# Loads and differences of ya and yb spread over the second in-projection, score banks held through the gated projections, and two low parts made later

## The chip, the cores and the metric

One core of a Trainium2 chip runs the whole kernel as one program. The metric is the device time of an execution in microseconds. TensorE is PE, VectorE DVE, ScalarE ACT, GpSimd POOL and SyncE SP; SP issues nearly all DMAs.

## The reference

A hybrid decoder block over 2048 positions of width 1024, all in f32:

```python
ada = (silu(c) @ w_ada + b_ada); shift, scale, gate = split(ada, 3)
h = rms(x, g_pre) * (1 + scale) + shift
q, k, v, z_a, u_b, v_b, z_b, g_logits = split(h @ w_in, SPLIT_IDX)
y_a = sliding_window_attention_with_sinks(rope(q), rope(k), v, sinks) * silu(z_a)
y_b = chunked_spatial_gating(gelu(u_b), gelu(v_b), ln_v_g, ln_v_b, w_s, b_s) * silu(z_b)
gate_a, gate_b = split(sigmoid(g_logits), 2)
merged = gate_a * (y_a @ w_proj_a) + gate_b * (y_b @ w_proj_b)
x = x + gate * rms(merged @ w_out, g_post)
```

q has 8 heads of 64, k and v have 2; the window is 128; u_b, v_b and z_b are 512 wide, the gate logits 2048. The spatial gating multiplies chunks of 128 positions of the layer-normalised v_b with a causal 128 x 128 matrix.

## The kernel before

**Products.** Every large product is made in parts of f32r: each operand is split into a high part (a rounded copy, made on ACT) and a low part (operand minus high part, made on DVE), and a tile takes three matmuls per 128 of depth: high by high, high by low, low by high (`mm3`, its matmul at L168). Blocks of products use seven multiplications instead of eight, with sums and differences of the quarters of both operands. One such multiplication is a *slot*: 12 matmuls of 128 x 512 into one PSUM bank, or six and six into two. There are 382 slots. `step` (L229) runs one; `later(n, f)` hangs an operation on the slot n further on, ahead of its matmuls, or behind them with `post`. Hooks are thus an order written by hand: the instructions of every engine stand in the order in which the hooks ran, and each engine and queue works through its own in order.

**Stages.** The rows are handled in two halves, s = 0 and s = 1. Each half has an in-projection of 133 slots. Beside its matmuls run, on hooks, the evacuation of its blocks, the layer norm of v_b (`ln_step`, L847: one load of vb at L850, transposes on PE at L856 four slots later), the transposes of k and v (L924, evacuated by ACT at L928), the rotary tables (`load_rope`, L791: 16 loads of 64 KB at L798), the spatial gating (loads of vn at L971, matmul at L977), and eight attention blocks (loads of q and k at L1019 and L1022, scores at L1038 and L1039 into the bank pair s, values at L1088). Then come the projections of y_a and y_b with their gates: for the rows of s = 0 in *pairs* (`Pair`), Pair 0 and Pair 1 of seven slots each, Pairs 2 and 3 interleaved in 14, and then `run_all`'s loop over j of 32 slots for the rows of s = 1, whose operands `T[0]` to `T[3]` are plain parts of ya and yb (`yab`). The out projection ends the kernel with 56 slots. The slots of s = 1 are counted here from the start of its in-projection: Pair 0 is 133 to 139, Pair 1 140 to 146, Pairs 2 and 3 147 to 160, the loop 161 to 192.

**Moving tiles.** `T[p]` is the moving operand of multiplication p, four k parts with a high and a low half. `t_load(T, p, n, srcs)` (L373) issues four loads of 256 KB into tiles of tag x, makes the four high parts on ACT (L384) at slots n, and the four low parts on DVE (L388, by `sub`, L151) at slots n + 1. Four of the seven operands of the pairs are sums and differences of quarters of the s = 0 part of ya and yb: `y_step(i)` (L1212) loads four x tiles of 256 KB, subtracts on POOL (`psub`, L154) into tiles of tag S, and stores four results to pT in DRAM. `presum` does the like for weights (four loads, POOL sums, four stores to sS), `o_step` for the output weights (stores to oT). `gate_step` and `gate_end` make the gate row rg.

**Buffers.** Tag x has 10 buffers, S 4, raw (loaded weights) 8, W (split weights) 4, T 7, e 6, m 4, q 5. PSUM holds the banks X, Y, Z, W, a rotating pair b, and one tile s of two banks. Weights are loaded some eight slots ahead of their use and split three slots ahead (L216 on ACT, L151 on DVE).

**Gating.** After a product of the pairs the block's banks are combined by adds on DVE (L157) into tiles e, multiplied with the gate (`gated`, L1236) and merged.

Of the kernel before, what the change touches and what calls it, by code (L numbers as in the profile page):

```python
# [8 lines left out]
F32 = mybir.dt.float32  # L9
# [6 lines left out]
P = 128  # L16
# [12 lines left out]
NPAIR = 19  # L29
# [26 lines left out]
def hybrid_block(ctx: ExitStack, tc: tile.TileContext, xt, x, wada, wgate, wI, wP, wO,  # L56
# [14 lines left out]
    def nm(s):  # L71
        uid[0] += 1
        return f"{s}_{uid[0]}"
# [22 lines left out]
    def bank():  # L96
        return pb.tile([P, 512], F32, tag="b", name=nm("b"))
# [124 lines left out]
    def later(n, f, post=False):  # L222
        hooks.setdefault((slot[0] + n, post), []).append(f)
# [77 lines left out]
    def p_quads(n):  # L301

        return {f"A{f + 1}{k + 1}": wP[2 * n + f][:, :, 256 * k : 256 * (k + 1)].rearrange("a p c -> p a c")
                for f in range(2) for k in range(2)}
# [65 lines left out]
    def t_new():  # L370
        return T_new().rearrange("p (a b c) -> p a b c", a=2, b=4)

    def t_load(T, p, n, srcs):  # L373

        rs = []
        for src in srcs:
            rs.append(flat("x"))
            sp.dma_start(rs[-1], src)

        def high(k0):  # L380
            if k0 == 0:
                T[p] = t_new()
            for kt in (k0, k0 + 1):
                act.copy(T[p][:, 0, kt, :], rs[kt])  # L384

        def low(k0):
            for kt in (k0, k0 + 1):
                sub(T[p][:, 1, kt, :], rs[kt], T[p][:, 0, kt, :].bitcast(F32))  # L388
        for i in range(2):
            later(n, lambda i=i: high(2 * i), i == 1)  # L390
            later(n + 1, lambda i=i: low(2 * i), i == 1)


    class Block:
# [767 lines left out]
    def o_step(kt):  # L1162
        hs = []
        for k in (kt, kt + 4):
            for h in range(2):
                hs.append(flat("x"))
                sp.dma_start(hs[-1], wO[k][:, h * 512 : (h + 1) * 512])
        keep_T(oT, kt, hs, False, 3)
# [43 lines left out]
    def y_step(i):  # L1212
        hs = []
        for k in (i % 2, i % 2 + 2):
            for h in range(2):
                hs.append(flat("x"))
                sp.dma_start(hs[-1], (ya_s, yb_s)[i // 2][h][:, k, :])
        keep_T(pT, i, hs, False, 3)
# [24 lines left out]
    def run_all():  # L1243
        nonlocal T

        for s in range(NS):
            uz = [{} for _ in range(4)]
            kinds = [lambda: ev_vb(s, 0), lambda: ev_vb(s, 2), lambda: ev_kv(s), lambda: ev_q(s, 0), lambda: ev_g(s, 0),
                     lambda: ev_q(s, 2), lambda: ev_za(s, 0), lambda: ev_za(s, 2)]
            kinds += [lambda c=c: ev_uz(s, c, uz[c]) for c in range(4)]  # L1250
            kinds += [lambda j=j: ev_g(s, j) for j in range(1, 8)]

            if s == 0:
                later(19, setup_sgu)
                later(22, zero_heads)
            later((18, 12)[s], lambda s=s: load_rope(s))
            for i in range(8):
                later((22, 17)[s] + 3 * i, lambda i=i: ln_step(s, i))
            for c in range(4):
                later(52 + 7 * c, lambda c=c: uz_load(s, c, uz[c]))  # L1260
            for i in range(8):
                for off, post, f in att_block(s * 8 + i):
                    later(62 + 8 * i + off, f, post)
            if s == 0:
                for i in range(8):
                    later(30 + 5 * i, lambda i=i: h1_stats(i))
                later(71, h1_rstd)
                for kt in range(4):
                    later(76 + 10 * kt, lambda kt=kt: h1_step(kt))
                for i in range(NLAST):  # L1270
                    later(91 + 10 * i, lambda i=i: presum(NPAIR - NLAST + i, wI_quads(NPAIR - NLAST + i)))
            else:
                for i in range(4):
                    later(6 + 3 * i, lambda i=i: y_step(i))
                for i in range(2):
                    later((1, 82)[i], lambda i=i: presum(NPAIR + i, p_quads(2 + i)))
                for kk in range(KT):
                    later(30 + 7 * kk, lambda kk=kk: gate_step(kk))
                for h in range(2):
                    later(87 + 4 * h, lambda h=h: gate_end(h))  # L1280
                for kt in range(4):
                    later(90 + 7 * kt, lambda kt=kt: o_step(kt))

            n0 = 0
            if s == 0:
                n0 = NFIRST
                S = pS.tile([P, 2, 512], F32, tag="s", name=nm("s"))
                bks = [two_banks(BK["X"], BK["W"]), two_banks(BK["Y"], BK["Z"]), two_banks(S[:, 0, :], S[:, 1, :])]
                blks = [Block(bks[i], kinds[i](), "mme"[i]) for i in range(NFIRST)]
                def second_half():  # L1290
                    rstd(1, BK["Z"])
                    ada_row(1, range(2))
                    rstd_out(1, BK["W"])
                    sum_to(2 * NFIRST + 2)
                    want(NFIRST)
                    ada_row(1, range(2, 8))
                    for i in range(6):
                        t_part(1, i)
                        if i == 2:
                            low_now()  # L1300
                            ada_rows_out(1)
                        elif i == 4:
                            want(NFIRST + 1)

                def second_rows():
                    low_now()
                    ada_fin(1)
                    want(NFIRST + 3)
                    for i in range(2):
                        t_part(2, i)  # L1310
                    low_now()
                    
                def fetch_all():
                    cur["cap"] = 1 << 30
                later(2, second_half, True)
                later(3, fetch_all, True)
                later(3, second_rows, "mid")
                later(3, lambda: sp.dma_start(mcpt, mcp))
                later(3, lambda: sp.dma_start(snk8, sinks.broadcast_to([P, 8])))
                later(9, lambda: dve.tensor_scalar(out=snk8, in0=snk8, scalar1=1.0 / SM, scalar2=None, op0=ALU.mult))  # L1320
                for i in range(2, 6):
                    later(3 + (i > 2), lambda i=i: t_part(2, i), i != 3)
                for p in range(3, 7):
                    for i, (n, post) in enumerate(((-3, True), (-3, True), (-2, False), (-2, True), (-1, False), (-1, True))):
                        later(3 * p + n, lambda p=p, i=i: t_part(p, i), post)
                for p in range(7):
                    for i in range(NFIRST):
                        w = w_get()
                        step(lambda: blks[i].run(p, w, T))
            for n in range(n0, NPAIR - NLAST):  # L1330
                blk = Block(BK, kinds[n]())
                for p in range(7):
                    w = w_get()
                    step(lambda: blk.run(p, w, T))
            bks = [two_banks(BK["X"], BK["W"]), two_banks(BK["Y"], BK["Z"])]
            blks = [Block(bks[i], kinds[NPAIR - NLAST + i]()) for i in range(NLAST)]
            nT = [None] * 7
            for p in range(7):
                if s == 0:
                    t_load(nT, p, 2, hT[p])  # L1340
                else:
                    t_load(nT, p, 2, p_src(p))
                for i in range(NLAST):
                    w = w_get()
                    step(lambda: blks[i].run(p, w, T))
            T = nT

        def banks():
            S = pS.tile([P, 2, 512], F32, tag="s", name=nm("s"))
            return S[:, 0, :], S[:, 1, :], bank(), bank()  # L1350

        for n in range(2):
            c = banks()
            blk = Pair(n, (BK, {"X": c[0], "Y": c[1], "Z": c[2], "W": c[3]}))
            for p in range(7):
                w = w_get()
                step(lambda: blk.run(p, w, T))
        c = banks()
        blks = [Pair(2, (two_banks(BK["X"], BK["W"]), two_banks(BK["Y"], BK["Z"]))),
                Pair(3, (two_banks(c[0], c[1]), two_banks(c[2], c[3])))]  # L1360
        nT = [None] * 7
        for p in range(7):
            if p < 4:
                t_load(nT, p, 2, yab(1, p))
            if p == 6:
                g_load(1, 0)
            for i in range(2):
                w = w_get()
                step(lambda: blks[i].run(p, w, T))
# [171 lines left out]
```

## Time and profile before

| what | value |
|---|---|
| time, median of 3 runs | 1227.82 us (1227.78 to 1229.73) |
| profiled execution | 1228.62 us |
| its span | 1226.9 us, so 1.72 us lie around it |
| mean granted clock of TensorE | 0.991 |
| busy: PE, DVE, ACT, POOL | 1199.8, 863.2, 631.8, 348.0 us |
| moved by DMA | 311.47 MB, mean 254 GB/s |

Times are of one profiled execution. PE's sum of busy time includes matmuls at a lower clock, so a loss can show as idle time or as long matmuls; the clock in a stretch of time tells the second. A row of the timeline gives start, length, engine, line, operation and operands, the count of like instructions run together, and in brackets the idle time ahead with what ended it. SPq is SP's DMA queue. A row of a table by stretches gives for each engine the busy time and count, and then the granted clock, the DMA engines' mean share and GB/s.

### The profile page before, as it was taken

To read this page: it belongs to the slowest core of one execution; us is meant where nothing else is said; L and a number is where in the kernel's file an instruction comes from. 1 tells how busy PE (TensorE), PEld (TensorE's weight loads), DVE (VectorE), ACT (ScalarE), POOL (GpSimd) and SP (SyncE) were. 2 spreads that over 40 slices of the span, in tenths; PEclk is the share of its full clock that TensorE was granted. 3 is DMA by queue.
4 is the path that set the end of the run, shared out by engine and by line. 5 is a ranking of instruction groups with operands and counts; after the bars stand their busy time and mean duration, and the time that the engine had idled before them with its cause. 6 is when DMAs were issued, how large, how long until landed. Compare 5 with 4: busy or idle time off the path is not lost.

```text
span 1226.9 us, 17364 instructions
## 1 busy us (share of the span) xinstructions
PE 1199.8 (98%) x5450; PEld 953.9 (78%) x5450; DVE 863.2 (70%) x1315; ACT 631.8 (51%) x1367; POOL 348.0 (28%) x294
## 2 busy tenths in 40 slices
PE   9999999999999999979999999999999899999997
PEld 3677887878777777868888787777778788888886
DVE  7996979568776575337775776555877957777675
ACT  4475455567765586424345675555845412444443
POOL 0002754224465201353300011111142310055443
PEclk9999999999999999989999999999999899999999
DMA  9545998967999998899788679889968898855452
GB/s 351 222 153 183 315 317 293 253 143 223 313 348 343 299 318 264 286 310 292 261 272 217 175 192 298 258 267 276 328 207 287 298 301 261 284 172 168 141 181 86
DMA packets 227828, 311.47 MB, mean 254 GB/s; under 512 B 20884, under 2 KB 102932, under 8 KB 227736
## 3 DMA queue, kind: packets, MB, share of 16 engines
q1 hardware_dynamic: 227264, 309.68, 78.2%
q8 instruction: 43, 0.70, 0.2%
q0 software_dynamic: 176, 0.53, 0.2%
q14 instruction: 49, 0.40, 0.1%
q10 hardware_dynamic: 296, 0.16, 0.0%
HBM read 200.51 MB, written 104.53 MB: 249 GB/s over the span
## 4 chain that ended last, share of the span: by engine, by line
PE 84%; DVE 6%; DMA 5%; ACT 2%; issue 1%; POOL 1%; SPq 0%; DVEq 0%; ACTq 0%; POOLq 0%
PE bankY L168 27%; PE bankX L168 19%; PE bankW L168 11%; PE bankZ L168 11%; PE s L168 4%; PE b L168 3%; PE b L1088 2%; PE s L1038 2%; DMA T<-in_wada 1%; PE s L1039 1%; DVE W L151 1%; PE b L977 1%; PE b L1073 1%; DMA raw<-sS 1%; DMA raw<-in_wI 1%
## 5 line engine op out<-in xcount | busy, mean ns | idle before, releaser
L168 PE MATMUL bankY<-T,W 128*128 128x512 f32 x1614 | 393.6, 392 | 0.9 <-ACT bankZ L429 0.6
L168 PEld LDWEIGHTS bankY<-T,W 128*128 128x128 f32 x1614 | 301.4, 188 | 64.7 <-ACT bankZ L429 1.0
L151 DVE TENSOR_TENSOR W<-raw,W 128x512 fp32r<-128x512 f32 x330 | 263.7, 804 | 81.4 <-ACT W L216 81.1
L168 PE MATMUL bankX<-T,W 128*128 128x512 f32 x1134 | 278.8, 393 | 1.8 <-DVE T L740 1.7
L216 ACT CAST W<-raw 128x512 fp32r<-128x512 f32 x330 | 203.6, 618 | 144.5 <-PE b L168 42.8
L168 PEld LDWEIGHTS bankX<-T,W 128*128 128x128 f32 x1134 | 210.0, 188 | 47.8 <-DVE T L740 5.0
L168 PE MATMUL bankW<-T,W 128*128 128x512 f32 x696 | 176.2, 400 | 3.2 <-DVE T L151 1.6
L168 PE MATMUL bankZ<-T,W 128*128 128x512 f32 x696 | 169.5, 392 | 0.0
L168 PEld LDWEIGHTS bankW<-T,W 128*128 128x128 f32 x696 | 130.5, 191 | 35.7 <-DVE T L151 3.2
L168 PEld LDWEIGHTS bankZ<-T,W 128*128 128x128 f32 x696 | 130.7, 189 | 27.1
L154 POOL TENSOR_TENSOR S<-x,x 128x512 f32<-128x512 f32 x28 | 37.5, 1345 | 304.2 <-DMA q<-q 119.4
L154 POOL TENSOR_TENSOR raw<-raw,raw 128x512 f32<-128x512 f32 x48 | 76.2, 1588 | 98.8 <-DVE W L151 47.0
L151 DVE TENSOR_TENSOR T<-x,T 128x512 fp32r<-128x512 f32 (+1 forms) x105 | 75.5, 762 | 8.5 <-ACT T L384 8.3
L154 POOL TENSOR_TENSOR S<-raw,raw 128x512 f32<-128x512 f32 x24 | 37.6, 1566 | 142.3 <-DMA raw<-in_wI 56.4
L157 DVE TENSOR_TENSOR e<-bankY,e 128x512 f32<-128x512 f32 x44 | 30.3, 689 | 65.2 <-PE bankY L168 65.2
L168 PE MATMUL s<-T,W 128*128 128x512 f32 x282 | 71.0, 396 | 4.5 <-DVE e L157 3.1
L168 PEld LDWEIGHTS s<-T,W 128*128 128x128 f32 x282 | 53.3, 191 | 16.9 <-issue 3.8
L154 POOL TENSOR_TENSOR raw<-S,raw 128x512 f32<-128x512 f32 x24 | 35.0, 1460 | 82.0 <-DVE W L151 62.4
L384 ACT CAST T<-x 128x512 fp32r<-128x512 f32 x100 | 55.9, 619 | 2.7 <-PE s L168 2.1
L1067 ACT ACTIVATE P<-P,rc 128x128 f32<-128x128 f32 x128 | 44.5, 396 | 10.2 <-DVE rc L1063 9.9
L429 ACT COPY bankZ<-bankY 128x512 f32<-128x512 f32 x42 | 24.0, 571 | 46.0 <-PE bankY L168 45.9
L408 ACT COPY e<-bankW 128x512 f32<-128x512 f32 x41 | 23.9, 584 | 44.7 <-PE bankW L168 42.1
(267 smaller groups left out, 1449.3 us busy)
## 6 DMA issues: line engine op xcount, KB each, us to landing
raw<-in_wI SPq DMA_DIRECT2D x128, 256.0 KB, 4.6
raw<-sS SPq DMA_DIRECT2D x92, 256.0 KB, 4.9
g<-e SPq DMA_DIRECT2D x64, 256.0 KB, 4.5
sS<-raw SPq DMA_DIRECT2D x45, 256.0 KB, 4.5
T<-in_wada SPq DMA_DIRECT2D x16, 512.0 KB, 8.2
q<-q SPq DMA_DIRECT2D x64, 128.0 KB, 5.6
q<-k_s SPq DMA_DIRECT2D x64, 128.0 KB, 5.4
raw<-m SPq DMA_DIRECT2D x32, 256.0 KB, 4.5
```

Source lines behind the costliest of these rows:

```text
L151: dve.tensor_tensor(out=o, in0=a, in1=b, op=ALU.subtract)
L154: pool.tensor_tensor(out=o, in0=a, in1=b, op=op)
L157: dve.tensor_tensor(out=o, in0=a, in1=b, op=ALU.add)
L168: pe.matmul(o, w[:, i, sl], t[:, j, kt, :], start=start and kt == kts[0] and n == 0, stop=stop and kt == last and n == 2, skip_group_check ...
L216: act.copy(w[:, 0, :], src)
L384: act.copy(T[p][:, 0, kt, :], rs[kt])
L408: act.copy(self.wsb, b["W"])
L429: act.copy(self.b[to], self.b[of])
L977: pe.matmul(b[:, ch * P : (ch + 1) * P], st["v", h][:, ch, :], wT[:, c, :], start=True, stop=True)
L1038: pe.matmul(o, q[:, g, :], k[:, 0, :], start=True, stop=False)
L1067: act.activation(out=st["P", kv][:, g, 0:P], in_=st["P", kv][:, g, 0:P], func=AF.Copy, scale=st["rc", kv][:, g : g + 1])
L1088: pe.matmul(o[own, :], v[:, k, own], st["pv", kv][k], start=k == 1, stop=k == 0)
```

## The change

Three edits. In the s = 1 in-projection the steps hang on other slots: y_step(0) to y_step(3) from 6, 9, 12, 15 to 64, 71, 1, 57; presum(0) and presum(1) from 1 and 82 to 78 and 83; gate_end from 87 and 91 to 91 and 98; o_step from 90, 97, 104, 111 to 94, 100, 106, 112. In the pairs, the tile s and two b banks are allocated once ahead of them instead of anew for each. And `t_load` takes an optional m: with it the low parts hang on slots m and m + 1, which is used with 8 for T[2] and T[3] in the interleaved pairs, so that these are made at slots 159 to 162 instead of from 154 and 156 on. The numbers of instructions on every engine stay the same.

```diff
-    def t_load(T, p, n, srcs):
+    def t_load(T, p, n, srcs, m=None):
...
         for i in range(2):
             later(n, lambda i=i: high(2 * i), i == 1)
-            later(n + 1, lambda i=i: low(2 * i), i == 1)
+            if m is None:
+                later(n + 1, lambda i=i: low(2 * i), i == 1)
+            else:
+                later(m + i, lambda i=i: low(2 * i))
...
                 for i in range(4):
-                    later(6 + 3 * i, lambda i=i: y_step(i))
+                    later((1, 57, 64, 71)[i], lambda i=i: y_step((2, 3, 0, 1)[i]))
                 for i in range(2):
-                    later((1, 82)[i], lambda i=i: presum(NPAIR + i, p_quads(2 + i)))
+                    later((78, 83)[i], lambda i=i: presum(NPAIR + i, p_quads(2 + i)))
                 for kk in range(KT):
                     later(30 + 7 * kk, lambda kk=kk: gate_step(kk))
                 for h in range(2):
-                    later(87 + 4 * h, lambda h=h: gate_end(h))
+                    later((91, 98)[h], lambda h=h: gate_end(h))
                 for kt in range(4):
-                    later(90 + 7 * kt, lambda kt=kt: o_step(kt))
+                    later(94 + 6 * kt, lambda kt=kt: o_step(kt))
...
-        def banks():
-            S = pS.tile([P, 2, 512], F32, tag="s", name=nm("s"))
-            return S[:, 0, :], S[:, 1, :], bank(), bank()
-
+        S = pS.tile([P, 2, 512], F32, tag="s", name=nm("s"))
+        c = S[:, 0, :], S[:, 1, :], bank(), bank()
         for n in range(2):
-            c = banks()
             blk = Pair(n, (BK, {"X": c[0], "Y": c[1], "Z": c[2], "W": c[3]}))
...
-        c = banks()
...
             if p < 4:
-                t_load(nT, p, 2, yab(1, p))
+                t_load(nT, p, 2, yab(1, p), 8 if p > 1 else None)
```

What this moves on the engines is shown at three places. Lines behind t_load are numbered three higher in the changed kernel.

SP's queue ahead of the first load of vb (line 850) in the s = 1 in-projection, before: y_step's loads from yb and its stores to pT stand between the weights (raw).

```order
L239 DMA raw_5185<-sS_1_91 128x512
L1217 DMA x_5187<-yb_294 128x512
L1217 DMA x_5189<-yb_295 128x512
L1217 DMA x_5191<-yb_294 128x512
L1217 DMA x_5193<-yb_295 128x512
L838 DMA pT_1_195<-S_5141 128x512
L239 DMA raw_5219<-in_wI 128x512
L838 DMA pT_1_203<-S_5164 128x512
L239 DMA raw_5240<-sS_2_92 128x512
L850 DMA q_5242<-vb_304 128x4x128
```

The same place in the changed kernel (the load of vb is at line 853):

```order
L239 DMA raw_5123<-sS_0_90 128x512
L841 DMA vb_304<-e_5118 128x512
L239 DMA raw_5142<-sS_1_91 128x512
L239 DMA raw_5163<-in_wI 128x512
L239 DMA raw_5181<-sS_2_92 128x512
L853 DMA q_5183<-vb_304 128x4x128
```

The loads of yb and the stores to pT are gone from there; weights and stores of vb are left.

SP's queue ahead of the q and k loads of the attention block whose values are loaded next to presum's new place at slot 78, before:

```order
L239 DMA raw_6989<-sS_1_127 128x512
L1027 DMA v_6991<-v_s 128x256
L239 DMA raw_7025<-in_wI 128x512
L1031 DMA e_7027<-za_288 128x4x128
L1019 DMA q_7037<-q_309 64x4x128 x2
L1022 DMA q_7040<-k_s 64x2x256 x2
```

And now:

```order
L239 DMA raw_6971<-sS_1_127 128x512
L1030 DMA v_6973<-v_s 128x256
L239 DMA x_6979<-in_wP 128x2x256
L239 DMA x_6981<-in_wP 128x2x256
L239 DMA x_6983<-in_wP 128x2x256
L239 DMA x_6985<-in_wP 128x2x256
L841 DMA pT_1_203<-S_6907 128x512
L239 DMA raw_7016<-in_wI 128x512
L1034 DMA e_7018<-za_288 128x4x128
L1022 DMA q_7028<-q_309 64x4x128 x2
L1025 DMA q_7031<-k_s 64x2x256 x2
```

presum(0)'s four loads (in_wP) and a store of y_step(1) have come in ahead of the q and k loads.

DVE in the interleaved pairs, before, up to the add that reads bank s: low parts of T[2] (T_9414) and T[3] (T_9476) stand between the weights' lows (W), gates and adds.

```order
L151 TENSOR_TENSOR T_9414<-x_9342,T_9414 128x512
L151 TENSOR_TENSOR T_9414<-x_9344,T_9414 128x512
L1236 SCALAR_TENSOR_TENSOR m_9383<-m_9383,s_9233 128x512
L1236 SCALAR_TENSOR_TENSOR q_9385<-q_9385,b_9234 128x512
L151 TENSOR_TENSOR T_9414<-x_9346,T_9414 128x512
L151 TENSOR_TENSOR T_9414<-x_9348,T_9414 128x512
L151 TENSOR_TENSOR W_9441<-raw_9290,W_9441 128x512
L157 TENSOR_TENSOR e_9496<-bankW,e_9307 128x512
...
L151 TENSOR_TENSOR T_9476<-x_9401,T_9476 128x512
L151 TENSOR_TENSOR T_9476<-x_9403,T_9476 128x512
L157 TENSOR_TENSOR e_9529<-s_9233,e_9334 128x512
```

The same stretch in the changed kernel:

```order
L1239 SCALAR_TENSOR_TENSOR m_9377<-m_9377,s_8886 128x512
L1239 SCALAR_TENSOR_TENSOR q_9379<-q_9379,b_8887 128x512
L151 TENSOR_TENSOR W_9435<-raw_9284,W_9435 128x512
L157 TENSOR_TENSOR e_9486<-bankW,e_9301 128x512
L157 TENSOR_TENSOR e_9487<-bankZ,e_9302 128x512
L1239 SCALAR_TENSOR_TENSOR S_9411<-S_9411,e_9486 128x512
L1239 SCALAR_TENSOR_TENSOR q_9413<-q_9413,e_9487 128x512
L151 TENSOR_TENSOR W_9462<-raw_9312,W_9462 128x512
L157 TENSOR_TENSOR e_9517<-s_8886,e_9328 128x512
```

The low parts are gone from ahead of the add; they stand ten adds and gates further on.

## The prediction

> **What bounds the kernel now.** I read the page's table of busy time first, then PE's waits, then the timeline round each long wait, and only then the engine or queue that PE was waiting for.
>
> ```profile
> PE 1199.8 (98%) x5450; PEld 953.9 (78%) x5450; DVE 863.2 (70%) x1315; ACT 631.8 (51%) x1367; POOL 348.0 (28%) x294
> ...
> PE b L856 <- DMA q<-vb: 4.2, 1, 4.2
> PE s L168 <- DVE e L157: 3.1, 1, 3.1
> PE b L924 <- ACT S L928: 3.1, 1, 3.1
> ```
>
> PE is the bound: 1199.8 of 1226.9 us. No matmul is added or removed, so the change can only touch two things: the 27 us in which PE idles, and the busy time that is long because the clock is low. Three waits hold 10.4 of the 27 us. The first and the third lie 9 us apart in the s = 1 in-projection (stall A); the second lies at the end of the gated projections (stall B). PE round stall A, each row with its start, its length, and in brackets its idle time:
>
> ```profile
> 523.00 2.89 PE L168 MATMUL bankY<-T,W 128*128 128x512 f32 x12
> 525.72 0.60 PE L924 MATMUL b<-cst,e 128*128 128x128 f32 x4
> 526.08 3.02 PE L168 MATMUL bankX<-T,W 128*128 128x512 f32 x12
> 533.28 1.09 PE L856 MATMUL b<-cst,q 128*128 128x128 f32 x4 [4.19 <-DMA q<-vb]
> 534.02 5.05 PE L168 MATMUL bankW<-T,W 128*128 128x512 f32 x12
> 542.19 1.12 PE L924 MATMUL b<-cst,e 128*128 128x128 f32 x4 [3.11 <-ACT S L928]
> 542.96 4.09 PE L168 MATMUL bankY<-T,W 128*128 128x512 f32 x12
> 546.88 2.89 PE L168 MATMUL bankX<-T,W 128*128 128x512 f32 x12
> ```
>
> At full rate a slot of 12 matmuls takes 525.72 - 523.00 = 2.72 us and four transposes 526.08 - 525.72 = 0.36. The three slots and two sets of transposes from 526.08 to 546.88 took 20.80 us and would take 3 x 2.72 + 2 x 0.36 = 8.88. So stall A costs 11.92 us: 7.30 idle and 4.62 in slow matmuls. The stretches of 5 us there (last columns: granted clock, DMA share, GB/s) show the second part:
>
> ```profile
> 530.00:535.00 5.00, 1.72 (x6) 1.58 (x7) 1.28 (x2) 0.62 (x1) 4.00 (x3) 0.66 0.93 329
> 535.00:540.00 5.00, 4.08 (x11) 2.84 (x9) 2.10 (x3) 0.00 (x0) 4.75 (x6) 0.65 0.97 307
> 540.00:545.00 5.00, 2.81 (x9) 2.42 (x10) 1.80 (x3) 3.10 (x6) 2.53 (x3) 0.69 1.00 348
> ```
>
> Why the transposes wait stands in SP's queue and on ACT:
>
> ```profile
> 500.72 10.75 SPq L798 DMA_DIRECT2D m<-cs  x16
> 511.51 2.00 SPq L1217 DMA_DIRECT2D x<-yb  x4
> 520.75 2.20 SPq L1217 DMA_DIRECT2D x<-yb  x4
> 526.67 0.90 SPq L850 DMA_DIRECT2D q<-vb  x1
> 541.55 0.58 ACT L928 COPY S<-b 128x512 f32<-128x512 f32 x1 [9.80 <-POOL x L154]
> ```
>
> The 16 loads of the rotary tables hold SP for 10.75 us, and behind them come eight loads of ya, yb and their stores to pT. The load of vb for ln_step(0) is due at slot 17, which is four slots before the slot that starts at 526.08, so at about 526.08 - 4 x 2.72 - 0.36 = 514.8; it is issued at 526.67. DMA engines are full from 530 to 545. The second transpose waits for a copy into an S tile, and the four S buffers are those of y_step's differences, whose stores are late for the same reason.
>
> Stall B, the same two views:
>
> ```profile
> 963.60 1.52 PE L168 MATMUL bankX<-T,W 128*128 128x512 f32 x6
> 964.96 1.52 PE L168 MATMUL bankY<-T,W 128*128 128x512 f32 x6
> 969.62 2.90 PE L168 MATMUL s<-T,W 128*128 128x512 f32 x6 [3.14 <-DVE e L157]
> ...
> 977.92 1.63 PE L168 MATMUL s<-T,W 128*128 128x512 f32 x6
> ...
> 965.00:970.00 5.00, 1.86 (x8) 1.31 (x7) 5.00 (x8) 0.62 (x1) 1.64 (x1) 0.85 0.75 274
> 970.00:975.00 5.00, 5.00 (x13) 3.84 (x13) 5.00 (x8) 0.00 (x0) 1.67 (x1) 0.50 0.64 188
> ```
>
> Half a slot (six matmuls) takes 964.96 - 963.60 = 1.36 us. The next s bank could start at 966.32, and four half slots later 977.92 would be 966.32 + 5.44 = 971.76. Stall B costs 6.16 us: 3.14 idle and 3.02 of low clock. DVE is busy for the whole of both stretches (5.00 of 5.00).
>
> **Part 1: the y_steps leave slots 6 to 15.** Three of the four y_steps (6 MB of loads and stores) go to slots 57, 64 and 71; y_step(2) takes the place of presum(0) at slot 1, 2 MB for 2 MB. Between the rotary loads and the first vb load stand, after the change, only weight loads and vb stores. The queue is through with the rotary loads at 511.5 and then reaches the vb load close to its due 514.8, some 10 us sooner than now; the transpose was 4.19 us short, so it has 5 us or more to spare. y_step(2)'s last S buffer is filled by slot 5, so the L928 copy finds one free. Both waits go, and with them their slow matmuls: -11.92 us. If the rotary loads alone still held the vb load, the 4.19 would stay in part; I give that a twentieth below.
>
> **Part 2: low parts of T[2] and T[3].** DVE ahead of the add that released PE:
>
> ```profile
> 957.10 2.40 DVE L151 TENSOR_TENSOR T<-x,T 128x512 fp32r<-128x512 f32 x2
> ...
> 960.62 2.38 DVE L151 TENSOR_TENSOR T<-x,T 128x512 fp32r<-128x512 f32 x2
> ...
> 966.52 2.35 DVE L151 TENSOR_TENSOR T<-x,T 128x512 fp32r<-128x512 f32 x2
> 968.80 0.68 DVE L157 TENSOR_TENSOR e<-s,e 128x512 f32<-128x512 f32 x1
> ```
>
> Six low parts, 7.13 us, stand ahead of that add in a queue that never idles. Without them it could end at 969.48 - 7.13 = 962.4, but its own inputs come later: the sums of bankW and bankZ can start near 960.9, five operations at 0.60 each follow, so the add runs from 963.9 to 964.5, 1.8 us ahead of 966.32. The add of the next s bank, ten operations at 0.60 later, ends near 970.6, 1.2 us ahead of 971.76. So -6.16 us. The eight low parts (2 x 2.40 per tile and stretched as before, 9.5 us in all) now stand at slots 159 to 162, where each slot has two gating operations and one weight low, 1.8 of 2.72 us. Laying DVE's new order end to end at 0.60 an operation and 1.20 a low part of T: T[2] is first read two slots after run_all begins (at 971.76 + 2.72 x 3 = 979.92), and its lows end near 978.7; T[3] one slot later, 982.64, its four k parts wanted at 982.9 to 984.9 and made at 982.2 to 984.0. That margin, some 0.7 us, is the thinnest of the change. Cost taken 0, up to +6 if it fails with the clock.
>
> **Part 3: the banks held.** The only wait it could remove:
>
> ```profile
> 918.38 1.66 PE L168 MATMUL s<-T,W 128*128 128x512 f32 x6 [1.39 <-DVE q L1236]
> ```
>
> This first matmul of Pair 1 into s waits for Pair 0's last gating to read the same two banks. Allocated once or per pair, it is the same memory with the same reader, so the wait stays: 0, with bounds of 0 and -1.39.
>
> **Part 4: what comes back at slots 56 to 112.** Four loads and four stores of 256 KB each (2.1 MB) with four POOL subtractions per y_step, and presum(0)'s at slot 78. The gate_end and o_step steps shift by 1 to 11 slots; their results are read tens of slots later (oT and the gate row in the last projection), so 0. The 23 to 24 us stretches that take the load in:
>
> ```profile
> 640.00:663.00 23.00, 23.00 (x119) 19.64 (x118) 13.13 (x21) 8.78 (x16) 0.00 (x0) 1.00 0.75 200
> 663.00:687.00 24.00, 23.96 (x124) 20.15 (x123) 15.36 (x28) 17.47 (x38) 0.00 (x0) 1.00 0.54 156
> 687.00:711.00 24.00, 24.00 (x121) 18.94 (x120) 16.55 (x31) 15.36 (x40) 0.00 (x0) 1.00 0.77 209
> 711.00:735.00 24.00, 24.00 (x121) 19.04 (x121) 19.41 (x34) 16.40 (x36) 4.92 (x4) 1.00 0.85 225
> ...
> q<-k_s SPq DMA_DIRECT2D x64, 128.0 KB, 5.4
> 715.83 1.21 SPq L1022 DMA_DIRECT2D q<-k_s  x2
> 729.08 0.39 PE L1038 MATMUL s<-q,q 128*128 128x256 f32 x1
> ```
>
> At 329 GB/s for a share of 0.93 a full machine moves 354 GB/s, so 2.1 MB is 5.9 us, 0.25 of a stretch: 0.75, 0.54, 0.77, 0.85 become 1.01, 0.79, 1.02, 1.10. At the worst the transfers run 0.10 x 24 = 2.4 us late. presum(0)'s four loads stand ahead of the q and k loads of the scores at 729.08 and add 1.05 MB, 3.0 us. Those loads land at 715.83 + 1.21 + 5.4 = 722.4, 6.6 us early; 5.4 us of lateness leaves 1.2. POOL's work slows DVE, as the weights' lows show with POOL idle (640 to 725) and busy (1085 to 1130):
>
> ```profile
> L151 DVE TENSOR_TENSOR W<-raw,W 128x512 fp32r<-128x512 f32 x24 | 16.3, 683 | 4.1 <-ACT W L216 4.1
> ...
> L151 DVE TENSOR_TENSOR W<-raw,W 128x512 fp32r<-128x512 f32 x14 | 13.8, 995 | 0.0
> ```
>
> Sixteen POOL operations that stretch one DVE operation each by 0.31 us make 5 us over 95 us in which DVE is busy 64.5: absorbed, except where an attention step has no spare time. I take +0.75 us for small idles, from bounds of 0 (all hidden) and +6.2 (one wait of stall B's size with its clock). A gain is excluded, since PE idles 0.04 us in these stretches.
>
> **The sum.** The profiled execution took 1228.62 us (span 1226.9 and 1.72 around it), 0.80 over the median 1227.82. 1228.62 - 11.92 - 6.16 - 0 + 0.75 = 1211.29, and against the median 1210.5.
>
> **A rule beside the rows.** A gap of 1.39 us at 918.38 left the next six matmuls at 1.66 us, nearly full rate; one of 3.14 us brought the clock to 0.50. So I charge an idle of 3 us about 6.2. The Trainium skill, "TensorE: Matmul & The Clock Gate", section "HAM oscillation — how this bites in real kernels", asks for no PE gaps over about 3.4 us. Read as a threshold it leaves stall B's 3.14 us without a clock cost, and the change would gain 3.02 us less, 1213.5; the 0.50 after that very gap speaks against it, and the row decides.
>
> **The rivals.**
> - One new stall in slots 57 to 90, most likely the scores at 729.08 or the steps at slots 65 to 72: for it speak shares of 1.0 to 1.1 and 1.2 us of margin; against it the 6.6 us that these loads have today. 1210.5 - 0.75 + 6.2 = about 1216. Chance 0.15.
> - T[3]'s lows late at slot 164: margin 0.7 us on a DVE queue whose T lows vary. +1 to +6: 1212 to 1216. Chance 0.09.
> - Slower than before: DMA becomes the bound of the attention. With shares over 1 from slot 57 on, lateness adds up, and once it passes the 6.6 us above, every block waits: scores, values and vn of four blocks at 6.2 us each, 24.8 us, gives 1235. It decides when a q load takes over 12 us to land (5.4 now). Against it: the 0.79 in the second stretch drains the backlog. Chance 0.04. With two or three blocks it is 1222 to 1228: 0.04.
> - Stall A goes only in part, the rotary loads alone delaying vb: one idle of 3 us with its clock stays, 1216.5. Against it: s = 0 has the same rotary loads, and the wait at L856 is counted once. Chance 0.05.
> - The change does more than I say: Pair 1's wait at 918.38 goes too, 1209.1. Chance 0.05. The threshold rule as a mechanism (clock cost not tied to the 3.14 us gap): 1213.5, chance 0.03.
>
> **How the numbers follow.** The forecast, 1210.5, has 0.55 (1209.7 to 1212). A measurement of this kernel tells 0.2%, 2.5 us, from no change. The range 1208.5 to 1218 holds forecast, banks, threshold, T[3] and most of the single stalls, some 0.85; above it lie the runs with several stalls. Faster 0.92, same 0.04 (three stalls), slower 0.04.
>
> **What would show it.** Right: no idle over 1 us on PE in slots 15 to 30 and granted clock 1.00 there; the vb load issued within 3 us of its slot; the s bank at slot 158 starting with no idle; the 1.4 us wait of Pair 1 still there; DMA share near 1 in slots 57 to 84 with PE idle under 2 us in all. Wrong: a wait of PE on q, x or v loads or on DVE in slots 57 to 90, or on T's lows at slot 163 or 164, with a clock under 0.9 behind it.

## The result and the profile after

The changed kernel takes 1211.63 us (1210.93 to 1212.11, 4 runs) against 1228.78 for the kernel before in the same measurement (1227.78 to 1229.92): ratio 0.986, 95% interval 0.9843 to 0.9877, so 15 to 19 us faster. The forecast was 1210.5. The profiled execution took 1210.93 us, its span 1209.2, 17.7 less than before.

The page's row of busy times, and of PE's waits the one that stayed, after:

```profile
PE 1191.1 (98%) x5450; PEld 948.9 (78%) x5450; DVE 864.4 (71%) x1315; ACT 631.7 (52%) x1367; POOL 355.2 (29%) x294
...
PE s L168 <- DVE q L1239: 1.4, 1, 1.4
```

With the same 5450 matmuls PE is busy for 8.7 us less; 7.64 of that is the slow matmuls of the two stalls (4.62 and 3.02). The waits on vb, on the S tile and on the add e are no longer in the list; the wait of Pair 1 for the gating is, with its 1.4 us. PE at the place of stall A, after:

```profile
526.52 3.02 PE L168 MATMUL bankX<-T,W 128*128 128x512 f32 x12
529.38 0.60 PE L859 MATMUL b<-cst,q 128*128 128x128 f32 x4
529.73 2.99 PE L168 MATMUL bankW<-T,W 128*128 128x512 f32 x12
532.56 0.60 PE L927 MATMUL b<-cst,e 128*128 128x128 f32 x4
532.91 3.02 PE L168 MATMUL bankY<-T,W 128*128 128x512 f32 x12
535.77 2.88 PE L168 MATMUL bankX<-T,W 128*128 128x512 f32 x12
```

No brackets, so no idle time, and no slot is long. From 526.52 to 535.77 it is 9.25 us where it was 20.80: 11.55 gained. The queue of SP ahead of it, and two stretches whose last columns are granted clock, DMA share and GB/s:

```profile
500.67 10.04 SPq L801 DMA_DIRECT2D m<-cs  x16
518.35 0.57 SPq L853 DMA_DIRECT2D q<-vb  x1
...
525.00:530.00 5.00, 5.00 (x27) 4.16 (x26) 1.23 (x2) 1.96 (x4) 0.00 (x0) 1.00 0.78 242
530.00:535.00 5.00, 5.00 (x25) 4.11 (x25) 4.04 (x6) 2.33 (x5) 3.90 (x4) 1.00 0.61 196
```

The rotary loads still take 10 us of SP, but the load of vb follows at 518.35 instead of 526.67, 11 us ahead of the transpose at 529.38. The place of stall B, after:

```profile
953.52 1.52 PE L168 MATMUL bankY<-T,W 128*128 128x512 f32 x6
954.88 1.52 PE L168 MATMUL s<-T,W 128*128 128x512 f32 x6
...
960.32 1.52 PE L168 MATMUL s<-T,W 128*128 128x512 f32 x6
```

From one s bank to the next but one it is 960.32 - 954.88 = 5.44 us, four half slots of 1.36, and the start at 954.88 is 1.36 after bankY's: 6.16 gained. 11.55 + 6.16 = 17.71 is the whole difference of the spans. That it fits to the hundredth is luck: 0.44 us lost ahead of stall A, 0.33 won between the two stalls and 0.10 won behind them cancel. Where the y_steps went, the stretches that answer to those of before (12 us earlier on the clock):

```profile
628.00:651.00 23.00, 23.00 (x116) 19.53 (x115) 14.02 (x20) 7.82 (x15) 5.88 (x4) 1.00 1.01 274
651.00:675.00 24.00, 24.00 (x126) 20.23 (x125) 17.99 (x31) 18.32 (x39) 5.91 (x4) 1.00 0.84 257
675.00:699.00 24.00, 24.00 (x119) 18.86 (x118) 17.50 (x30) 13.41 (x33) 4.79 (x4) 1.00 0.96 273
699.00:723.00 24.00, 24.00 (x124) 19.17 (x123) 16.73 (x31) 16.68 (x41) 6.60 (x5) 1.00 0.89 246
```

The DMA engines are about as full as expected in the first three stretches and less full in the last, and PE is busy for 95.00 of 95 us.

### The profile page after: what moved, and what is told of

Its sections match the earlier page's. It is cut to its first block, busy times and chain, and to the rows that moved or that the text cites. A ratio compares the mean times of both kernels' runs of the same rounds, so it can differ in the third digit from the quotient of the medians.

```text
span 1209.2 us, 17368 instructions
## 1 busy us (share of the span) xinstructions
PE 1191.1 (98%) x5450; PEld 948.9 (78%) x5450; DVE 864.4 (71%) x1315; ACT 631.7 (52%) x1367; POOL 355.2 (29%) x294
## 4 chain that ended last, share of the span: by engine, by line
PE 89%; DVE 7%; ACT 2%; issue 1%; POOL 0%; DVEq 0%; ACTq 0%; POOLq 0%
PE bankY L168 28%; PE bankX L168 20%; PE bankW L168 12%; PE bankZ L168 12%; PE s L168 4%; PE b L168 3%; PE b L1091 2%; PE s L1041 2%; PE s L1042 1%; DVE W L151 1%; PE b L980 1%; DVE e L157 1%; PE b L1076 1%; DVE T L743 1%; PE b L681 1%
## 5 line engine op out<-in xcount | busy, mean ns | idle before, releaser
L151 DVE TENSOR_TENSOR W<-raw,W 128x512 fp32r<-128x512 f32 x330 | 271.6, 827 | 70.6 <-ACT W L216 70.4
L168 PE MATMUL bankW<-T,W 128*128 128x512 f32 x696 | 173.1, 395 | 3.4 <-DVE T L743 2.5
L151 DVE TENSOR_TENSOR T<-x,T 128x512 fp32r<-128x512 f32 (+1 forms) x105 | 69.6, 708 | 8.5 <-ACT T L384 8.3
```

The costliest lines, as they stand in the source:

```text
L151: dve.tensor_tensor(out=o, in0=a, in1=b, op=ALU.subtract)
L168: pe.matmul(o, w[:, i, sl], t[:, j, kt, :], start=start and kt == kts[0] and n == 0, stop=stop and kt == last and n == 2, skip_group_check ...
```

## The experiments

Times are medians beside the kernel before on the same chip. What a ratio leaves open is given in us as its interval.

**One part at a time.** e1 is the kernel before with the new slots only, e2 with the late low parts only, e3 with the banks held only.

```diff
-                    later(6 + 3 * i, lambda i=i: y_step(i))
+                    later((1, 57, 64, 71)[i], lambda i=i: y_step((2, 3, 0, 1)[i]))
...
```

> The kernel before with the new slots for y_step, presum, gate_end and o_step alone. Theory (two separate stalls, additive): stall A goes, -11.5 to -12 us, and stall B with its 3.1 us idle and low clock stays; about 1216 to 1217 if before is 1228. Rival (the gain comes from one cause, the second stall only follows from the first): about 1211, with stall B gone as well.

1216.78 against 1228.65, ratio 0.9903 (0.989 to 0.9915): -11.9 us. Neither the wait on vb nor that on S is among PE's waits, and stall B stands as before:

```profile
953.11 1.52 PE L168 MATMUL bankY<-T,W 128*128 128x512 f32 x6
957.75 2.71 PE L168 MATMUL s<-T,W 128*128 128x512 f32 x6 [3.12 <-DVE e L157]
960.26 2.07 PE L168 MATMUL b<-T,W 128*128 128x512 f32 x6
...
966.04 1.61 PE L168 MATMUL s<-T,W 128*128 128x512 f32 x6 [0.97 <-DVE e L157]
```

So the two stalls are separate. Stall B is as long as before: from 953.11 to 966.04 it is 12.93 us where five half slots take 6.80, so 6.13 are lost. But its make-up differs: slow matmuls take 1.7 us of it and not 3.02, and PE waits for DVE a second time, 0.97 us, at the next s bank.

```diff
...
-                t_load(nT, p, 2, yab(1, p))
+                t_load(nT, p, 2, yab(1, p), 8 if p > 1 else None)
```

> The kernel before with only the low parts of T[2] and T[3] made later. Theory: stall B goes, -6.0 to -6.2 us, stall A stays at 7.3 us idle; about 1222 if before is 1228. Rival (another DVE operation takes over at the s bank, DVE being full there): -3 us or less, PE waiting at slot 160 or 164.

1220.30, ratio 0.9931 (0.9918 to 0.9944): -8.5 us, 6.9 to 10.1. Stall B's idle and low clock are gone, which is 6.2 us; the rest lies in stall A, which this edit does not touch:

```profile
525.69 3.02 PE L168 MATMUL bankX<-T,W 128*128 128x512 f32 x12
531.94 1.09 PE L859 MATMUL b<-cst,q 128*128 128x128 f32 x4 [3.24 <-DMA q<-vb]
...
539.94 0.66 PE L927 MATMUL b<-cst,e 128*128 128x128 f32 x4 [1.98 <-ACT S L931]
...
544.87 2.90 PE L168 MATMUL bankX<-T,W 128*128 128x512 f32 x12
```

Here it took 544.87 - 525.69 = 19.18 instead of 20.80 us. Stall A is not the same in every execution: in the traces of three other kernels that leave it alone it took 20.36 (e3), 20.56 (e6) and 18.34 us (e11), and the kernel before ranges over 5 us in 17 runs of this measurement (1226.35 to 1231.39), the changed one over 1.2. Why it came out short with e2 is not settled. e1 and e2 together (11.9 + 8.5) give 3.2 us more than the whole change (17.2); 1.6 of these are the shorter stall A of this trace, and the intervals are wide enough to hold the rest.

```diff
-        def banks():
...
+        S = pS.tile([P, 2, 512], F32, tag="s", name=nm("s"))
+        c = S[:, 0, :], S[:, 1, :], bank(), bank()
```

> The kernel before with only the tile s and the two b banks allocated once for the pairs. Theory: no difference (within 0.3 us), Pair 1's first matmul into s still waits 1.4 us for the gating. Rival (a new allocation costs a wait that holding avoids): -1.4 us, that wait gone.

1228.14, ratio 0.9996 (0.9987 to 1.0004): no difference. Pair 1's first matmul into s:

```profile
917.72 1.66 PE L168 MATMUL s<-T,W 128*128 128x512 f32 x6 [1.38 <-DVE q L1236]
```

The wait is what it was. To see what it waits for, e8 takes the changed kernel and exchanges two of the four banks, so that the bank written first in a pair lies in another tile than the one read last:

```diff
-        c = S[:, 0, :], S[:, 1, :], bank(), bank()
+        c = S[:, 0, :], bank(), S[:, 1, :], bank()
```

> The changed kernel with the second and third of the four banks exchanged, so that the banks X and Y of the second half of a pair lie in different tiles (s and b). Theory (the 1.4 us wait of Pair 1 is a dependence on the tile s as a whole, not on the bank that is written): that wait goes, -1.0 to -1.4 us against the changed kernel, about 1210.3. Rival (the bank itself is still being read): the wait stays, or comes back elsewhere in the pairs as a wait on b: 0 or worse.

1210.10 (1209.53 to 1210.35), ratio to before 0.9845 (0.9832 to 0.9857), where the changed kernel had 0.986. The same place in the trace of e8:

```profile
902.89 1.52 PE L168 MATMUL b<-T,W 128*128 128x512 f32 x6
...
905.61 1.52 PE L168 MATMUL s<-T,W 128*128 128x512 f32 x6
...
910.02 1.65 PE L168 MATMUL bankY<-T,W 128*128 128x512 f32 x6 [0.17 <-ACT bankY L493]
```

Slot 139 now ends in bank b, and bank s starts in slot 140 without idle time; 0.3 us comes back two slots later. The dependence was on the tile s as a whole. The medians of e8 and of the changed kernel are 1.5 us apart, in two measurements whose kernels before agree (1228.65 and 1228.78), and the intervals of their ratios overlap. That the wait is gone is shown; that the time falls with it is likely, but not shown. e8 has the lowest median of this study.

**What stall A was made of.** e4 leaves the y_steps where they were and moves the rotary loads ahead of them; e5 takes v's copies out of the S buffers; e10 does both.

```diff
-            later((18, 12)[s], lambda s=s: load_rope(s))
+            later((18, 2)[s], lambda s=s: load_rope(s))
```

> The kernel before with the 16 loads of the rotary tables of s = 1 issued at slot 2 instead of 12; the y_steps stay at slots 6 to 15. Theory A1 (SP's order: the load of vb is issued late because 10.75 us of rotary issues and the y_steps' loads and stores stand ahead of it): the load of vb is issued some 10 us earlier, both idles of stall A shrink to under 1 us, -8 to -12 us. Theory A2 (the DMA engines are full with 6 MB of differences in these slots, whatever the order): the wait on vb or on S stays at 3 us or more, gain under 5 us.

1222.43 (1219.48 to 1224.27), ratio 0.995 (0.9932 to 0.9968): -6.2 us, between the two theories. The load of vb is issued at 521.29, 5.4 us earlier and not 10. The first wait is gone, the second is not:

```profile
528.86 0.60 PE L856 MATMUL b<-cst,q 128*128 128x128 f32 x4
...
535.58 0.66 PE L924 MATMUL b<-cst,e 128*128 128x128 f32 x4 [3.38 <-ACT S L928]
```

So both waits need naming: SP's order holds the first, and something else the second.

```diff
-                        o = flat("qS"[s])
+                        o = flat("q")
```

> The kernel before with the copies of v's transposes in s = 1 put into a tile of tag q instead of S. Theory (the second idle of stall A, 3.11 us, is only the S buffers that y_step's late stores hold): that idle goes and its share of the low clock, -3 to -5 us, the first idle of 4.2 us stays. Rival (the transposes are late through the same queue anyway, or q's buffers are as scarce): within 1.5 us of before.

1224.92, ratio 0.9971 (0.9961 to 0.9981): -3.6 us, as the theory had it; the mirror of e4:

```profile
534.41 1.09 PE L856 MATMUL b<-cst,q 128*128 128x128 f32 x4 [4.35 <-DMA q<-vb]
535.15 4.94 PE L168 MATMUL bankW<-T,W 128*128 128x512 f32 x12
539.92 0.60 PE L924 MATMUL b<-cst,e 128*128 128x128 f32 x4
```

The second wait was the four S buffers.

```diff
-            later((18, 12)[s], lambda s=s: load_rope(s))
+            later((18, 2)[s], lambda s=s: load_rope(s))
...
-                        o = flat("qS"[s])
+                        o = flat("q")
```

> The kernel before with both of the two single repairs of stall A: rotary loads at slot 2 and the copies of v's transposes in tiles of tag q; the y_steps stay at slots 6 to 15. Theory (stall A is two waits with two causes, SP's order behind the rotary loads and the S buffers, and not DMA that is full): both waits gone, -11 to -12 us, about 1217, as with the y_steps moved. Rival (6 MB in these slots are too much for the DMA engines): a wait of 2 us or more stays on vb, x or weights, gain under 9 us.

1217.42, ratio 0.9905 (0.9886 to 0.9924): -11.7 us, the same as e1, without a y_step moved. Its stretches of 10 us over the place:

```profile
505.00:515.00 10.00, 10.00 (x46) 8.29 (x45) 5.08 (x6) 4.46 (x8) 2.99 (x2) 1.00 1.02 341
515.00:525.00 10.00, 10.00 (x46) 8.29 (x45) 3.91 (x6) 3.46 (x6) 5.13 (x4) 1.00 1.02 353
525.00:535.00 10.00, 10.00 (x52) 8.26 (x51) 6.00 (x7) 4.30 (x8) 8.16 (x6) 1.00 0.96 326
535.00:545.00 10.00, 10.00 (x48) 8.28 (x47) 8.32 (x12) 3.34 (x6) 4.54 (x7) 1.00 1.03 344
```

The DMA engines are full for these 40 us and PE does not idle at all. A full DMA share was no cause of stall A; the order of SP's queue and a scarce tag were.

**Whether it matters where the y_steps go.**

```diff
-                    later((1, 57, 64, 71)[i], lambda i=i: y_step((2, 3, 0, 1)[i]))
+                    later((1, 66, 69, 72)[i], lambda i=i: y_step((2, 3, 0, 1)[i]))
```

> The changed kernel with its three late y_steps crowded into slots 66, 69 and 72, three slots apart as before the change, instead of 57, 64 and 71; 6 MB then fall among the attention blocks in some 10 slots. Theory (the loads there have several us to spare and the spacing matters): one or two waits of PE on q, k, x or S of 1 to 4 us, +2 to +8 us against the changed kernel. Rival (what counts is only to be away from the rotary loads and the vb loads): no difference within 1 us.

1221.40 (1219.47 to 1223.19), ratio 0.994 (0.992 to 0.9959): 10 us of the gain are lost, more than the theory's 2 to 8. PE waits longest for an add on DVE and not for the tiles that the theory named, but the chain behind that wait goes back to two of them, x and S. PE, DVE, SP and POOL in e9, and two stretches:

```profile
700.30 4.71 PE L168 MATMUL bankY<-T,W 128*128 128x512 f32 x12 [6.42 <-DVE e L157]
...
698.23 0.75 DVE L985 SCALAR_TENSOR_TENSOR x<-b,col,Tt 128x512 f32<-128x512 f32 x1 [15.05 <-POOL S L154]
...
686.93 6.52 SPq L974 DMA_DIRECT2D x<-vn  x2
...
696.93 1.26 POOL L154 TENSOR_TENSOR S<-x,x 128x512 f32<-128x512 f32 x1 [3.87 <-DMA pT<-S]
...
690.00:695.00 5.00, 3.88 (x20) 3.04 (x20) 0.00 (x0) 0.00 (x0) 1.29 (x1) 1.00 0.55 184
695.00:700.00 5.00, 0.00 (x0) 0.00 (x0) 1.77 (x4) 0.30 (x1) 1.26 (x1) 0.72 0.69 228
```

POOL's differences wait for S buffers whose stores to pT are not done; until POOL has read its x tiles, no x buffer is free; SP stands for 6.5 us at a load of vn that needs one, and DVE for 15 us at an operation of the spatial gating that writes one. Behind that operation in DVE's order is the add for which PE waits. The DMA engines are not full meanwhile (0.55, 0.69). So it matters where the y_steps go, and it does so through buffers. How much of it is the spacing and how much the place is not told apart: e9 changes both, and `gate_step` at slots 65 and 72 also takes S buffers.

**Stall B in parts.** First, what ends stall B. Before, this is the add on DVE that frees the second s bank:

```profile
977.09 0.68 DVE L157 TENSOR_TENSOR e<-s,e 128x512 f32<-128x512 f32 x1
```

It ended at 977.77, and PE began to write that bank at 977.92. So PE could not have begun much sooner at any clock. e4 leaves stall B alone, and its trace has the stall without a slow matmul:

```profile
957.11 1.52 PE L168 MATMUL bankY<-T,W 128*128 128x512 f32 x6
961.76 1.63 PE L168 MATMUL s<-T,W 128*128 128x512 f32 x6 [3.13 <-DVE e L157]
...
970.07 1.63 PE L168 MATMUL s<-T,W 128*128 128x512 f32 x6 [1.13 <-DVE e L157]
...
960.00:965.00 5.00, 3.24 (x14) 2.55 (x14) 5.00 (x8) 0.20 (x1) 1.51 (x1) 1.00 0.66 214
```

From 957.11 to 970.07 it is 12.96 us where five half slots take 6.80: 6.16 lost at a clock of 1.00, as much as before with its clock of 0.50. In place of the slow matmuls PE waits for DVE twice more, 1.16 us for a weight's low part and 1.13 for the second add. DVE takes 8.29 us from the first of the two adds to the second before, and 8.31 in e4. So DVE's queue sets the length of stall B, and the slow matmuls only fill time in which PE would have waited for DVE.

```diff
...
+                t_load(nT, p, 2, yab(1, p), 8 if p > 2 else None)
```

> The kernel before with only T[3]'s low parts made later, T[2]'s as before. One pair of low parts (2.35 us) less stands ahead of the add for which PE waits 3.14 us. Theory (the loss of clock belongs to an idle of about 3 us and does not come with one under 1.4): idle of 0.8 us, clock near 1.0, so -5.0 to -5.4 us of stall B's 6.16. Rival (the clock falls in proportion to the idle): idle 0.8 and low clock 0.8, -4.6 us; second rival (each bank waits in turn, the second add being late as well): -2.4 us.

1224.45, ratio 0.9967 (0.9957 to 0.9978): -4.1 us, 2.7 to 5.3. By the trace, three small idles replace one (0.51 on a copy of ACT, 0.86, 0.32), 1.7 us in all and not 0.8, and the clock is 1.00 throughout. Counted by the starts of the banks, the eleven half slots from the bank Z ahead of the first of these idles lose 2.5 us, where they lost 6.5 before: 4.0 less, as measured. No slow matmul came with these idles, as the theory had it. The gain does not test that, since the low clock was not what stall B cost. The second s bank waits for its add again (0.32), as the second rival had it, but more is won than the rival's 2.4.

```diff
...
+        if split3:
+            later(n + 1, lambda: low1(0))
+            later(8, lambda: low1(1))
+            later(9, lambda: low(2))
...
```

> The kernel before with T[3]'s first low part left in its place and its other three made later, so that one low part less (1.2 us) stands ahead of the add of stall B. Theory (a low clock comes only with an idle near 3 us): idle of about 2 us, clock 1.0, so stall B costs about 2.2 instead of 6.2, -4 us. Rival (the clock falls with any idle over 1.4 us): idle 2 and 2 to 3 of low clock, -1.2 to -2 us.

1226.94, ratio 0.9982 (0.9971 to 0.9993): -2.2 us, 0.9 to 3.6. The first s bank:

```profile
967.14 1.62 PE L168 MATMUL s<-T,W 128*128 128x512 f32 x6 [2.52 <-DVE e L157]
968.61 1.52 PE L168 MATMUL b<-T,W 128*128 128x512 f32 x6
```

The idle is 2.52 us, not 2: the one low part that is left took 1.75 us, where the two had taken 2.35. The matmuls behind it run at full rate in this trace, which is of the fastest of ten executions (1223.89). But the 4 us of the theory did not come of that. The next s bank starts at 973.15, after a wait of 0.30 for its add, so stall B still loses 3.25 us, 2.9 less than before. That lies within the measured interval and the theory's 4 does not; -1.2 to -2, which the rival forecast, does, but by a low clock that this trace does not show.

```diff
-                t_load(nT, p, 2, yab(1, p), 8 if p > 1 else None)
+                t_load(nT, p, 2, yab(1, p), (None, None, 8, 9)[p])
```

> The changed kernel with T[3]'s low parts one slot later still (162 and 163). Theory (margin of the changed kernel at slot 164 is 0.7 to 1.2 us, less than a slot of 2.72): PE waits 1.5 to 2 us at slot 164 for a low part of T[3], +1.5 to +2 us, without loss of clock as the idle is under 3. Rival (margin larger than the estimate): no idle, no difference.

1210.97, ratio 0.9861 (0.9846 to 0.9876), the same as the changed kernel. No wait on T's lows appears. The rival was right: the margin is larger than estimated.

## Why the prediction was right

The forecast was a gain of 17.3 us, and the medians give 17.2, the traces 17.7. Both stalls went, and what was moved was what held them. Two errors of opposite sign cancel in part: stall A gave 0.37 us less than its term, and the 0.75 us charged for the new load did not come.

**Stall A** was sized at 11.92 and gave 11.55 in the profile; the slots beside transposes take 2.86 rather than 2.72 us. Its mechanism held, SP's order for the first wait (e4) and S buffers for the second (e5). The prediction listed full DMA engines among the signs without giving them a share; e10 shows that they had none. The vb load came 3.1 us behind its slot (518.35 against 526.52 - 11.24 = 515.3), just past the 3 us allowed. SP was free from 514.8 on and waited there for a store of vb to land (3.5 us in the list of SP's waits), so what was left was no longer the order of its queue.

**Stall B** was sized at 6.16 and gave 6.16, and DVE's queue was named rightly. The split into 3.14 of idle and 3.02 of low clock was wrong as an account of the cost: the second add holds the next s bank for as long at a clock of 1.00 (e4). Before, six low parts stand ahead of the first add and two more ahead of the second; with T[3]'s four alone gone, 2.5 us are still lost (e6). The add that released PE ended at 952.34 + 0.69 = 953.0, 1.9 us ahead of need; estimated was 1.8. The second ended at 959.0, 1.3 us ahead, where 1.2 was expected. DVE's rows after:

```profile
952.34 0.69 DVE L157 TENSOR_TENSOR e<-s,e 128x512 f32<-128x512 f32 x1
...
958.34 0.69 DVE L157 TENSOR_TENSOR e<-s,e 128x512 f32<-128x512 f32 x1
...
961.34 1.30 DVE L151 TENSOR_TENSOR T<-x,T 128x512 fp32r<-128x512 f32 x2
...
967.34 2.51 DVE L151 TENSOR_TENSOR T<-x,T 128x512 fp32r<-128x512 f32 x4
```

**The margin of T[3]**, some 0.7 us, was mis-sized. The low parts were reckoned at 1.20 us each, as before the change; they took 0.65 and 0.63. T[3]'s four k parts were done from about 968.0 to 969.85. Slot 164 began at 971.20 and, by the prediction's own count, wants them from 0.26 to 2.26 us later, so the margin was some 3.5 us. e7's slot of 2.72 fits in that.

**The banks** were put at 0, and e3 measured 0. The reason given was half right: it is the same reader, but of the same tile and not of the same banks (e8).

**The new load** was put at 0.75 us; PE idled 0.00 in those stretches. The DMA shares expected were 1.01, 0.79, 1.02 and 1.10, those measured 1.01, 0.84, 0.96 and 0.89. The slower rival named DMA as the bound to come. The nearest thing to it that a run showed, e9, is a chain through tags S and x with DMA half idle; that the spacing of seven slots keeps the change clear of it was not in the prediction.

**The rule of the clock.** The prediction charged an idle of 3 us with about 6.2, and reckoned that the change would gain 3.02 us less, 1213.5, if no low clock belonged to the 3.14 us. That working did not hold. e4 loses 6.16 us at stall B without a low clock, so the change would have gained the same either way, and the measured 1211.63 does not decide between the two. "TensorE: Matmul & The Clock Gate" of the Trainium skill (section "HAM oscillation — how this bites in real kernels") asks for no PE gaps over about 3.4 us. Taken as a sharp threshold, that does not fit the trace of before, whose clock fell to 0.50 behind 3.14 us.

## What to carry to other kernels

When PE waits on a load, look first at where the load stands in its queue and which tag the data goes through, and only then at bandwidth: here DMA engines at a share near 1.0 for 40 us came with no idle of PE (e10), while sixteen small loads in front of one due load and four buffers for two users together cost 12 us. When work is moved into a fuller stage, give its steps the spacing at which each tag is returned before the next step asks for it. Before a low clock behind a wait is added to the price of the wait, look at what releases the next step: at stall B that was DVE, and the 3 us of slow matmuls cost nothing of their own.

## What the runs showed of the hardware

The length of an idle does not alone decide the clock. Idles of 3.12 to 3.14 us at stall B brought slow matmuls in five traces (before, e1, e3, e5, e10). One of 3.13 at the same place in e4 did not, one of 2.52 (e11) did not, and one of 3.38 at stall A in e4 did not either, as the stretch behind it shows:

```profile
535.00:540.00 5.00, 4.42 (x21) 3.68 (x22) 3.22 (x4) 3.91 (x8) 3.05 (x3) 1.00 0.98 291
```

The traced execution of e4 has a mean granted clock of 0.998, its four others 0.992 to 0.995. So it may be that the low clock comes in some executions of the same kernel and not in others; those four have no trace, and what decides it stays open.

Where low parts of T on DVE and subtractions on POOL ran at once, one of the two was slowed, and which one changed. Before, with two low parts of T at 960.62 in 2.38 us, POOL's subtraction kept its length; after, the low parts took 1.30 and POOL's was long:

```profile
960.77 1.68 POOL L154 TENSOR_TENSOR m<-m,q 128x512 f32<-128x512 f32 x1 [2.43 <-DVE q L1236]
```

After:

```profile
960.91 2.89 POOL L154 TENSOR_TENSOR m<-m,q 128x512 f32<-128x512 f32 x1 [1.32 <-DMA q<-g]
```

Not every overlap slows: in the changed kernel a weight's low part at 957.74 kept its 0.69 us, and POOL's subtraction at 957.91 its 1.68. What decides it is open.
